# Attention scores from rounded and rest parts in two fp32r products, and six modulation blocks moved to the second layer's attention

## The chip, the cores and the metric

The kernel runs on one core of a Trainium2 chip. The metric is the device time of one execution in microseconds. Before the change it is 2171.98 us, the median of three runs (2163.36, 2171.98 and 2172.99).

## The reference, cut to what matters

Two layers of a hybrid block work on 256 latent tokens and 256 context tokens of width 1024. Each layer computes a modulation vector from a condition, mixes tokens with an attention of eight heads of 64 and a gated delta recurrence of four heads of 128, and ends in a feed-forward part: dense in the first layer, a mixture of eight experts in the second. Everything is fp32.

```python
m_l = (jax.nn.silu(c) @ w_mod[l] + b_mod[l])[:, None, :]      # 6 x 1024 per layer, from 1024 x 6144 weights
m_c = (jax.nn.silu(c_ctx) @ w_mod[l] + b_mod[l])[None, None, :]
sh1, sc1, g1, sh2, sc2, g2 = jnp.split(m_l, 6, axis=-1)
...
s_loc = einsum(q_blk, k_blk) * scale + bias                   # a latent query sees 256 latent keys with a bias
s_ctx = einsum(q_blk, kc) * scale                             # and 256 context keys
p = softmax(concatenate([s_loc, s_ctx], -1))
...
s = einsum('bqhd,bkhd->bhqk', q, k) * (q.shape[-1] ** -0.5)   # context queries: 256 context keys, first layer only
```

The six parts of the modulation are used at different places: the first two ahead of the mixer, `g1` at its end, `sh2` and `sc2` behind it, and `g2` at the end of the feed-forward part. Of the second layer, blocks 0 to 5 of 512 columns hold the first three parts and blocks 6 to 11 the last three.

## The kernel before, in words

Activations are held transposed, with a feature on each partition, as two fp32r tiles for the rounded part and the rest. Weights come in loads of 1 MB through SP's DMA queue into one of three buffers (`raw`), are split by ScalarE (rounding, L90) and VectorE or GpSimd (rest, L91) into fp32r pairs (`ws`, two buffers), and are multiplied in three fp32r products (`mm3`): high times low, high times high, low times high.

A mixer does this work. The projections of the recurrence (`heads`) and of the attention (`fill_pair` for q and k, `fill_tok` for v and z) go through PSUM tiles of tag "acc" (two buffers). The recurrence needs a triangular inverse: `triangles`, a `substitution` of 31 steps on VectorE and GpSimd, `doubling` with small products, and then the steps `recur` and `delta_out`, which load kx, vt, qT and IN from DRAM through SP. `attention` runs per head and per tile of 128 queries: the score product (`sps`, tag "acc"), the bias and scale, maximum and exponential on VectorE and ScalarE, four transposes (`ptp`, tag "tp", two buffers), a copy to SBUF (`pt`), and the product with v (`aop`, tag "m" with one buffer in the second layer, "tp" in the first). The first layer has eight heads times four query tiles, two with 512 keys and two with 256; the second layer has eight heads times two tiles with 512 keys.

A modulation block (`mod_block`) loads two pieces of 1 MB without splitting them, multiplies them in 16 recorded fp32 products into a PSUM tile of tag "m", copies that on ScalarE (`mev`), transposes it in four products (`mt`, the same tag) and reduces it on VectorE. Four blocks run at the very beginning. The other 20 stand in `mod_queue`, and `mod_next` takes the next one, or nothing once the queue is empty. It is called for each of six pairs of the recurrence's projections in the first layer, for each of the 16 steps of the first layer's attention, and at several places of the dense part.

The order of the work is made in three stages. `drive` steps the recurrence and the doubling in turns, and after each turn takes a number of units from one generator, `stream`, that holds the projections, the attention (one unit per head and pair of query tiles) and z; what is left over is taken after them. The emitted order gives each instruction a priority. The framework then simulates a timeline with its own costs and gives each engine a fixed order from it: the first in priority of those that are ready. Buffers are given out by that simulation too. On the chip each engine, and SP's queue, goes strictly through its list.

SBUF tiles of 512 fp32 elements come from one pool (`big`, 48 buffers of 2 KB a partition, L175). The MoE's fifteen load buffers lie partly on the addresses of this pool and of those behind it; a load into one of them waits until what lay there has been read.

Lines that the steps below touch: `mod_queue` and the pool (L173 to L175), `fill_pair` (L404 to L413), the score product (L859), `aop` (L876), the call behind each head (L883 to L885), and the calls in the dense part (L1110, L1135, L1140).

Of the kernel before, what the change touches and what calls it, by code (L numbers as in the profile page):

```python
# [9 lines left out]
F32 = mybir.dt.float32  # L10
F32R = mybir.dt.float32r
I32 = mybir.dt.int32
AF = mybir.ActivationFunctionType
ALU = mybir.AluOpType
# [4 lines left out]
P = 128  # L19
# [35 lines left out]
class Kern:  # L55
# [78 lines left out]
    def run(self):  # L134
        nc, tc, I = self.nc, self.tc, self.I
        with ExitStack() as top:
            self.const = c = self.pool(top, "const")
            self.dram = top.enter_context(tc.tile_pool(name="scr", bufs=1, space=DRAM))
            self.cst = c.tile([P, 5, P], F32, name="cst")
            self.st = self.pool(top, "st", bufs=4)  # L140
            self.raw = self.pool(top, "raw", bufs=3)
            self.wsp = self.pool(top, "wsp", bufs=2)
            self.ps = self.pool(top, "ps", bufs=2, space=PSUM)
            pre = top.enter_context(ExitStack())
            early = self.pool(pre, "early")
            cT = early.tile([P, KD, 32], F32, name="cT")
            nc.vector.memset(cT, 0.0)
            craw = early.tile([P, KD, 2], F32, name="craw")
            nc.scalar.dma_start(craw, I["c"])
            nc.scalar.dma_start(self.cst, I["cst"])  # L150
            self.ident = self.cst[:, 0]
            self.tri = (self.cst[:, 1], self.cst[:, 2])
            self.stri = (self.cst[:, 3], self.cst[:, 4])
            nc.scalar.activation(cT[:, :, 0:2], craw, AF.Silu)
            self.cT = cT
            self.bm = early.tile([P, 2, 48], F32, name="bm")
            nc.scalar.dma_start(self.bm, I["b_mod"])
            self.rope = early.tile([P, 2, 2, 128], F32, name="rope")
            self.lnT = c.tile([P, 4, 2, KD], F32, name="lnT")
            nc.scalar.dma_start(self.lnT, I["lnT"])  # L160
            self.mods = [c.tile([P, 48, 2], F32, name=f"mod{l}") for l in range(2)]
            self.mhalf = c.tile([P, 16], F32, name="mhalf")
            nc.vector.memset(self.mhalf, -0.5)
            one = c.tile([P, 1], F32, name="one")
            nc.vector.memset(one, 1.0)
            self.ones = one.broadcast_to([P, P])
            self.pads = [early.tile([P, 2, 260], F32, name=f"pad{i}") for i in range(2)]
            for t in self.pads:
                nc.vector.memset(t[:, :, 0:2], 0.0)
                nc.vector.memset(t[:, :, 258:260], 0.0)  # L170
            self.x1_d = self.dram.tile([4, P, D], F32, name="x1d")
            self.x2_d = self.dram.tile([4, P, D], F32, name="x2d")
            self.mod_queue = [(0, n) for n in range(4, 12)] + [(1, n) for n in range(12)]  # L173
            with pre:
                self.pb = self.pool(pre, "big", bufs=48)  # L175
                self.pt = self.pool(pre, "tr", bufs=7)
                self.pc = self.pool(pre, "ch", bufs=4)
                self.pd = self.pool(pre, "db", bufs=6)
                self.pa = self.pool(pre, "at", bufs=2)
                self.pr = self.pool(pre, "ro", bufs=2)  # L180
                X = self.xtiles()
                xt = [[self.big(name="xt") for _ in range(2)] for i in range(4)]
                nc.gpsimd.dma_start(self.rope, I["rope"])
                steps = [self.xpose_mod(*self.mod_cols(0, 0, w), w, xt[2 * w : 2 * w + 2], X) for w in range(2)]

                for hf in range(2):
                    for n in (hf, 2 + hf):
                        self.mod_block(0, n)
                    for j in ((0, 1), ())[hf]:
                        for i in range(4):  # L190
                            nc.sync.dma_start(xt[i][j], I["xtok"][i][:, 512 * j : 512 * j + 512])
                        if j == 0:
                            self.first = list(self.wsplit(self.load(I["w_in"][0, 2]), eng=[nc.gpsimd] * 2))
                    for _ in range(4):
                        for t in steps:
                            next(t)
                X2, tail = self.mixer(0, X, None)
                X, tail = self.ffn(X2, tail)
                x1, ab = self.mixer(1, X, tail, top)
            self.moe(x1, ab)  # L200
# [78 lines left out]
    def mixer(self, l, X, tail, keep=None):  # L279
# [4 lines left out]
        with ExitStack() as mx:  # L284
# [117 lines left out]
            ftag, lo = ["g"], [None, None]  # L402

            def fill_pair(pair):  # L404
                to, w = (qa, NT * P) if pair < 8 else (ka, 512)
                r = self.load(I["w_in"][l, pair])
                t2 = self.big((P, 2, 256), name="qk") if w == 256 else None
                for j, hl in enumerate(self.wsplit(r, eng=lo)):
                    acc = wblock(hl, 0, w, ftag[0])
                    t = self.big((P, w), name="qk") if t2 is None else t2[:, j]  # L410
                    nc.scalar.copy(t, acc[:, 0:w])
                    to[2 * (pair % 2) + j] = t
                    yield  # L413

            def fill_tok(which, ch, nt):
# [430 lines left out]
    def attention(self, l, heads, tl, qaT, kaT, VA, na):  # L846
        nc = self.nc
        for h in heads:
            hp = slice(64 * (h % 2), 64 * (h % 2) + 64)
            hs = slice(64 * h, 64 * h + 64)  # L850
            if tl[0] == 0:
                bias = self.inp([P, 2, 256], "bias")
                nc.sync.dma_start(bias, self.I["rpb"][l, h])
            for i in tl:
                c0 = 0 if i < 2 else 256
                w = 512 - c0
                nk = w // P
                sp = self.pst("acc", name="sps")[:, 0:w]
                self.mm(sp, qaT[h // 2][hp, i * P : (i + 1) * P], kaT[h // 2][hp, c0:512], start=True, stop=True)  # L859
                st = self.st.tile([P, 4], F32, name="st", tag="st")  # L860
                pr = self.s2([P, 512], name="pr")
                if i < 2:
                    nc.vector.scalar_tensor_tensor(pr[:, 0:256], sp[:, 0:256], 0.125, bias[:, i], ALU.mult, ALU.add)
                    nc.scalar.activation(pr[:, 256:512], sp[:, 256:512], AF.Copy, scale=0.125)
                    nc.vector.tensor_reduce(st[:, 0:1], pr, AX.X, ALU.max, negate=True)
                    nc.scalar.activation(pr, pr, AF.Exp, bias=st[:, 0:1], accum_out=st[:, 1:2])
                else:
                    nc.vector.tensor_reduce(st[:, 0:1], sp, AX.X, ALU.max)
                    nc.vector.tensor_scalar(st[:, 2:3], st[:, 0:1], -0.125, None, ALU.mult)
                    nc.scalar.activation(pr[:, 0:w], sp, AF.Exp, scale=0.125, bias=st[:, 2:3], accum_out=st[:, 1:2])  # L870
                tp = self.pst("tp", (P, 4, P), name="ptp")
                for j in range(nk):
                    nc.tensor.transpose(tp[:, j], pr[:, j * P : (j + 1) * P], self.ident)
                pt = self.pa.tile([P, 4, P], F32, name="pt", tag="a")
                nc.any.tensor_copy(pt[:, 0:nk], tp[:, 0:nk])
                op = self.pst("m" if l else "tp", (P, 64), name="aop")  # L876
                vs = slice(64 * (h % 4), 64 * (h % 4) + 64)
                for j in range(nk):
                    kt = 4 - nk + j
                    self.mm(op, pt[:, j], VA[kt // 2][:, kt % 2, vs], start=j == 0, stop=j == nk - 1)  # L880
                nc.vector.reciprocal(st[:, 3:4], st[:, 1:2])
                nc.vector.tensor_scalar(na[i][:, hs], op, st[:, 3:4], None, ALU.mult)
            if l == 0:  # L883

                self.mod_next()  # L885
            yield

# [184 lines left out]
    def ffn(self, X, tail):  # L1072

        nc, I = self.nc, self.I
        m = self.mods[0]
        for half in range(2):
            H = []
            for f in range(11):
# [28 lines left out]
                nc.scalar.activation(sg, accs[0], AF.Silu)  # L1107
                nc.vector.tensor_tensor(sg, sg, accs[1], ALU.mult)
                self.split(H[f][0], H[f][1], sg)
                if f % 2:  # L1110
                    self.mod_next()
            if half == 0:
                xs = self.rows(self.x1_d, range(4))
                gr = [self.row(0, 40, w, lambda hf: self.big(name="gr")) for w in range(2)]
# [2 lines left out]
            for w in (None,) if half == 0 else (1, 0):  # L1117
# [4 lines left out]
                for hf in range(2):  # L1122
                    tags = (("acc", "acc", "tp", "tp"), ("g", "g", "g", "tp"))[hf] if w is None else ("acc", "g")[hf : hf + 1] * 2
                    acc = [self.pst(t, name="dacc") for t in tags]
                    for sl in range(3):
                        wd = 2048 if sl < 2 else 1536
                        r = self.load(I["w_dn"][half, hf, :, 2048 * sl : 2048 * sl + wd])
                        for j, (wh, wl) in enumerate(self.wsplit(r, wd)):
                            for q in range(min(2, wd // 512 - 2 * j)):
                                k = 4 * sl + 2 * j + q  # L1130
                                s = slice(512 * q, 512 * q + 512)
                                for a, i in zip(acc, tl):
                                    h = [t[:, i * P : (i + 1) * P] for t in H[k]]
                                    self.mm3(a, *h, wh[:, s], wl[:, s], k == 0, k == 10)
                        if sl:  # L1135
                            self.mod_next()
                    for n, (a, i) in enumerate(zip(acc, tl)):
                        self.residual(xs[i][hf], a, gr[i // 2][hf], 1.0 if half else ALPHA, st[n][:, hf] if half else None)
                if w == 1:
                    self.mod_next(12)  # L1140
                    run(steps)
        return X2, steps

# [730 lines left out]
```

## Time and profile before

| | |
|---|---|
| median of three runs | 2171.98 us |
| profiled execution | 2169.23 us, of which the span of the trace is 2167.4 us |
| TensorE matmul / weight load busy | 2009.4 us (93%) / 1382.7 us (64%) |
| VectorE / ScalarE / GpSimd busy | 1174.2 (54%) / 833.3 (38%) / 245.9 us (11%) |
| mean granted TensorE clock | 0.954 of full speed |
| DMA | 539.94 MB, mean 249 GB/s |

The span falls into these parts: the first layer's projections and inverse to about 240 us, its attention with the recurrence to 426, its output and the dense part to about 900, the second layer's mixer to about 1216, and the mixture of experts to the end. Matmuls are pipelined, so a busy time of TensorE is the union of records that each contain some latency. A granted clock of 1.00 is 2.4 GHz throughout a stretch, 0.50 would be 1.2 GHz throughout it.

### The profile page before, as it was taken

The numbers are of one execution on the slowest core, as the hardware profiler recorded it, in microseconds if no ns is written. First come the engines' busy times: TensorE is split into PE (matmuls) and PEld (weight loads), VectorE is DVE, ScalarE is ACT, GpSimd is POOL, SyncE is SP. The second block draws the span as 40 slices with busy tenths as digits, with TensorE's granted clock in tenths as the row PEclk, the third lists the DMA queues.
The fourth block names the chain that finished last, engine by engine and source line by source line (L and its number), as shares of the span: only waits on it lengthen the run. The fifth ranks groups of instructions, "written<-read, shape, count | busy, mean of one in ns | idle before, by whom it ended". The sixth has DMA issues, their size and how long they took to land. (4 is left out here: it accounts for less than half of the span.)

```text
span 2167.4 us, 29352 instructions
## 1 busy us (share of the span) xinstructions
PE 2009.4 (93%) x11334; PEld 1382.7 (64%) x11334; DVE 1174.2 (54%) x1980; ACT 833.3 (38%) x1312; POOL 245.9 (11%) x276
## 2 busy tenths in 40 slices
PE   7989999998999999898899889999999999998996
PEld 3678766777888887677768663555544445554553
DVE  3777455676324337867765671544344444455565
ACT  2454333443322234454344450433233434435451
POOL 1422200114000000536311000000000000000000
PEclk9999999898999999998789999999999999999998
DMA  8355387453323225334323689999999989989884
GB/s 325 129 192 159 134 308 289 151 203 102 135 93 109 97 91 185 109 111 129 111 76 117 270 349 405 426 427 426 427 374 405 412 325 427 367 317 425 328 333 167
DMA packets 121029, 539.94 MB, mean 249 GB/s; under 512 B 28560, under 2 KB 40912, under 8 KB 62512
## 3 DMA queue, kind: packets, MB, share of 16 engines
q1 hardware_dynamic: 118704, 532.35, 63.9%
q0 software_dynamic: 1600, 5.20, 0.7%
q8 instruction: 91, 1.49, 0.3%
q14 instruction: 58, 0.48, 0.1%
q10 hardware_dynamic: 576, 0.42, 0.1%
HBM read 520.10 MB, written 17.83 MB: 248 GB/s over the span
## 5 line engine op out<-in xcount | busy, mean ns | idle before, releaser
L91 DVE TENSOR_TENSOR ws<-raw,ws 128x1024 fp32r<-128x1024 f32 (+1 forms) x384 | 461.5, 1224 | 261.9 <-ACT ws L90 260.7
L90 ACT CAST ws<-raw 128x1024 fp32r<-128x1024 f32 (+1 forms) x404 | 412.8, 1043 | 338.9 <-PE ga L75 102.2
L75 PE MATMUL ga<-ws,xe 128*128 128x512 f32 x1008 | 261.8, 416 | 32.4 <-DVE ws L91 32.4
L75 PE MATMUL ga<-raw,xr 128*32 128x512 f32 (+1 forms) x1568 | 261.2, 601 | 0.7 <-ACT xr L1371 0.7
L75 PEld LDWEIGHTS ga<-ws,xe 128*128 128x128 f32 x1008 | 195.6, 198 | 100.0 <-DVE ws L91 40.0
L75 PE MATMUL facc<-xh,ws 128*128 128x512 f32 (+1 forms) x736 | 224.0, 386 | 1.9 <-DVE ws L91 1.8
L75 PE MATMUL acc<-xh,ws 128*128 128x512 f32 (+1 forms) x672 | 202.8, 385 | 8.0 <-DVE ws L91 5.4
L75 PEld LDWEIGHTS facc<-xh,ws 128*128 128x128 f32 x736 | 139.6, 193 | 28.9 <-DVE ws L91 2.6
L75 PEld LDWEIGHTS ga<-raw,xr 128*32 128x32 f32 (+1 forms) x1568 | 69.7, 121 | 138.0 <-issue 129.8
L75 PEld LDWEIGHTS acc<-xh,ws 128*128 128x128 f32 x672 | 129.5, 205 | 34.2 <-DVE ws L91 6.1
L75 PE MATMUL facc<-xl,ws 128*128 128x512 f32 (+1 forms) x368 | 143.0, 389 | 2.0 <-ACT ws L90 1.5
L75 PE MATMUL acc<-xl,ws 128*128 128x512 f32 (+1 forms) x336 | 131.5, 391 | 10.4 <-ACT va L435 5.9
L75 PE MATMUL dacc<-ws,Hh 128*128 128x512 f32 x352 | 109.3, 392 | 2.8 <-DVE ws L91 2.8
L75 PE MATMUL y<-ws,hh 128*128 128x512 f32 x336 | 107.5, 401 | 0.0
L1574 POOL TENSOR_TENSOR mv<-mv,mhalf 128x1 f32<-128x1 f32 x2 | 2.0, 993 | 891.0 <-DVE mv L1573 889.2
L75 PE MATMUL yf<-raw,hr 128*32 128x512 f32 (+1 forms) x560 | 93.5, 616 | 2.5 <-ACT hr L1754 2.5
L75 PEld LDWEIGHTS acc<-xl,ws 128*128 128x128 f32 x336 | 69.0, 205 | 26.9 <-ACT va L435 6.3
L75 PE MATMUL acc<-ws,xh 128*128 128x256 f32 x448 | 83.2, 286 | 0.0
L91 DVE TENSOR_TENSOR hl<-tp,hh 128x512 fp32r<-128x512 f32 x21 | 14.5, 692 | 125.5 <-ACT hh L90 125.4
L75 PEld LDWEIGHTS facc<-xl,ws 128*128 128x128 f32 x368 | 71.3, 194 | 16.4 <-ACT ws L90 2.1
L75 PEld LDWEIGHTS dacc<-ws,Hh 128*128 128x128 f32 x352 | 65.1, 188 | 17.6 <-DVE ws L91 4.2
L75 PEld LDWEIGHTS y<-ws,hh 128*128 128x128 f32 x336 | 62.9, 190 | 21.0 <-DVE ws L91 4.1
(372 smaller groups left out, 3005.6 us busy)
## 6 DMA issues: line engine op xcount, KB each, us to landing
raw<-in_m_gu_dram SPq DMA_DIRECT2D x224, 1024.0 KB, 12.3
raw<-in_m_dn_dram SPq DMA_DIRECT2D x112, 1024.0 KB, 13.4
raw<-in_w_mod_dram SPq DMA_DIRECT2D x44, 1024.0 KB, 4.9
raw<-in_w_in_dram SPq DMA_DIRECT2D x28, 1024.0 KB, 5.1
raw<-in_w_gu_dram SPq DMA_DIRECT2D x22, 1024.0 KB, 4.8
raw<-in_w_out_dram SPq DMA_DIRECT2D x12, 1024.0 KB, 4.8
raw<-in_w_dn_dram SPq DMA_DIRECT2D x12, 1024.0 KB, 4.9
raw<-in_w_dn_dram SPq DMA_DIRECT2D x6, 768.0 KB, 4.3
```

The source lines that it names most:

```text
L75: self.next(self.nc.tensor.matmul(*a, **k))
L90: eng.tensor_copy(hi, src) if both else self.nc.scalar.copy(hi, src)
L91: (eng or self.nc.vector).tensor_tensor(lo, src, hi.bitcast(F32), ALU.subtract)
L1574: nc.gpsimd.tensor_tensor(mv[:, 1:2], mv[:, 1:2], self.mhalf[:, 0:1], ALU.pow)
```

## The change

The score of one head becomes two fp32r products that accumulate into the same PSUM tile. For a k tile (two heads, 64 features each, on the two halves of the partitions) `fill_pair` now makes two tiles, one for each head: the rounded part of the head on its own half, the rest on the other half. For a q tile it makes three: for each head the rounded part on both halves, and a third with the rests of both heads on their own halves. The first product contracts over 128 partitions (rounded q times rounded k, and rounded q times the rest of k), the second over 64 (the rest of q times rounded k). The product of the two rests is left out. The copies are ScalarE's, the subtractions VectorE's.

The `big` pool gets 57 buffers instead of 48. The tile `aop` takes tag "tp" in both layers. The modulation queue is drawn on differently: the first layer's attention takes a block behind a head only while more than six are left, and behind each odd head only while more than twelve are left; the second layer's attention takes one behind each head. The calls in the dense part are gone.

```diff
-                self.pb = self.pool(pre, "big", bufs=48)
+                self.pb = self.pool(pre, "big", bufs=57)
...
             def fill_pair(pair):
-                to, w = (qa, NT * P) if pair < 8 else (ka, 512)
+                q = pair < 8
+                to, w = (qa, NT * P) if q else (ka, 512)
                 r = self.load(I["w_in"][l, pair])
-                t2 = self.big((P, 2, 256), name="qk") if w == 256 else None
+                halves = (slice(0, 64), slice(64, 128))
+                small = w == 256
+                both = [self.big((P, 2, 256), F32R, name="qk") for _ in range(3)] if small else None
                 for j, hl in enumerate(self.wsplit(r, eng=lo)):
                     acc = wblock(hl, 0, w, ftag[0])
-                    t = self.big((P, w), name="qk") if t2 is None else t2[:, j]
-                    nc.scalar.copy(t, acc[:, 0:w])
-                    to[2 * (pair % 2) + j] = t
+                    n = 3 if q else 2
+                    ts = [both[m][:, j] if small else self.big((P, w), F32R, name="qk") for m in range(n)]
+                    for m in range(2):
+                        mine, other = halves[m], halves[1 - m]
+                        t, a = ts[m], acc[mine, 0:w]
+                        nc.scalar.copy(t[mine], a)
+                        if q:
+                            nc.scalar.copy(t[other], a)
+                        rest = ts[2][mine] if q else t[other]
+                        nc.vector.tensor_tensor(rest, a, t[mine].bitcast(F32), ALU.subtract)
+                    to[2 * (pair % 2) + j] = ts
                     yield
...
-                self.mm(sp, qaT[h // 2][hp, i * P : (i + 1) * P], kaT[h // 2][hp, c0:512], start=True, stop=True)
+                q, k, tok = qaT[h // 2], kaT[h // 2][h % 2], slice(i * P, (i + 1) * P)
+                self.mm(sp, q[h % 2][:, tok], k[:, c0:512], start=True, stop=False)
+                self.mm(sp, q[2][hp, tok], k[hp, c0:512], start=False, stop=True)
...
-                op = self.pst("m" if l else "tp", (P, 64), name="aop")
+                op = self.pst("tp", (P, 64), name="aop")
...
-            if l == 0:
+            if l == 1 or len(self.mod_queue) > 6 and (h % 2 == 0 or len(self.mod_queue) > 12):
                 self.mod_next()
...
-                if f % 2:
-                    self.mod_next()
...
-                        if sl:
-                            self.mod_next()
...
-                    self.mod_next(12)
                     run(steps)
```

## Rows read from the trace of the kernel before

**Rows 1.** Busy us: PE, PEld, DVE, ACT, POOL; granted clock, DMA share, GB/s.
```profile
268.00:414.00 146.00, 146.00 (x1230) 97.97 (x1229) 81.73 (x245) 57.23 (x149) 9.24 (x13) 1.00 0.76 278
414.00:426.00 12.00, 9.41 (x49) 7.85 (x47) 5.69 (x16) 3.81 (x9) 1.64 (x1) 0.63 0.01 1
...
1000.00:1040.00 40.00, 34.36 (x243) 32.62 (x241) 37.08 (x71) 14.48 (x24) 28.07 (x43) 0.90 0.43 133
1040.00:1072.00 32.00, 25.88 (x230) 23.32 (x230) 23.17 (x52) 14.57 (x39) 10.23 (x10) 0.69 0.41 123
1072.00:1120.00 48.00, 43.71 (x322) 32.50 (x322) 25.61 (x67) 18.59 (x46) 5.28 (x8) 0.74 0.28 88
1120.00:1143.00 23.00, 23.00 (x213) 17.98 (x213) 18.25 (x49) 11.52 (x29) 2.40 (x4) 1.00 0.05 13
...
1220.00:1240.00 20.00, 15.48 (x95) 12.76 (x94) 13.05 (x45) 10.46 (x18) 2.53 (x7) 0.83 0.99 410
1240.00:1260.00 20.00, 13.43 (x51) 10.50 (x50) 15.39 (x28) 9.28 (x10) 0.54 (x1) 0.83 0.58 220
```

**Rows 2.** Timeline of TensorE, first layer's attention: start us, duration us.
```profile
363.67 0.60 PE L227 MATMUL mt<-cst,mev 128*128 128x128 f32 x4
364.11 1.28 PE L75 MATMUL sp<-vn,kx 128*128 128x128 f32 x10
...
366.54 1.92 PE L75 MATMUL mps<-raw,cT 128*32 128x512 f32 x16
368.40 1.13 PE L75 MATMUL sps<-qk 64*128 64x256 f32 x4
369.45 0.56 PE L75 MATMUL qt<-YT,NP 64*64 64x64 f32 x6
...
375.49 1.98 PE L75 MATMUL sps<-qk 64*128 64x512 f32 x4
377.40 0.71 PE L75 MATMUL op<-vn,IN 128*128 128x128 f32 x4
```

**Rows 3.** Timeline of TensorE: fp32r products, dense layer and z.
```profile
523.25 0.39 PE L75 MATMUL facc<-xl,ws 128*128 128x512 f32 x1
...
523.93 0.39 PE L75 MATMUL facc<-xl,ws 128*128 128x512 f32 x1
...
1144.01 0.40 PE L75 MATMUL acc<-ws,xh 128*128 128x256 f32 x2
...
1144.37 0.40 PE L75 MATMUL acc<-ws,xh 128*128 128x256 f32 x2
```

**Rows 4.** Groups by line and shape, ScalarE then VectorE.
```profile
L411 ACT COPY qk<-acc 128x512 f32<-128x512 f32 x12 | 6.8, 595 | 5.0 <-PE acc L75 4.9
...
L411 ACT COPY qk<-acc 128x256 f32<-128x256 f32 x4 | 1.4, 372 | 8.3 <-PE acc L75 8.3
...
L91 DVE TENSOR_TENSOR hl<-tp,hh 128x512 fp32r<-128x512 f32 x21 | 14.5, 692 | 125.5 <-ACT hh L90 125.4
...
L91 DVE TENSOR_TENSOR xe<-gp,xe 128x256 fp32r<-128x256 f32 x12 | 4.8, 420 | 4.2 <-ACT xe L90 4.2
```

**Rows 5.** Timeline of TensorE, tail of the first layer's attention.
```profile
420.08 1.97 PE L75 MATMUL aop<-va,pt 128*128 128x64 f32 x8 [0.73 <-ACT pt L875]
```

**Rows 6.** Timeline of SP's DMA issues, both layers.
```profile
329.74 30.66 SPq L98 DMA_DIRECT2D raw<-in_w_mod_dram  x8
...
1043.13 0.34 SPq L98 DMA_DIRECT2D raw<-in_w_in_dram  x1
1046.67 0.35 SPq L98 DMA_DIRECT2D raw<-in_w_out_dram  x1
...
1081.55 12.54 SPq L318 DMA_DIRECT2D qd<-cv  x2
...
1094.70 0.40 SPq L736 DMA_DIRECT2D kx<-kd  x1
```

**Rows 7.** Timeline of SP's DMA issues, start of the MoE's loads.
```profile
1166.57 13.31 SPq L98 DMA_DIRECT2D raw<-in_m_gu_dram  x2
```

## The prediction

> **What bounds the kernel now.** I read four views in this order: the busy table by stretches, then TensorE's timeline in the first layer's attention, then the DMA queue of SP, then the groups of ScalarE and VectorE copies.
>
> The table by stretches [rows 1] shows two very different attentions. In the first layer's (268 to 414 us) TensorE is busy for 146.00 of 146.00 us at a granted clock of 1.00, VectorE for 81.73 and ScalarE for 57.23; DMA is at 0.76. Every one of the 14 modulation blocks that this attention carries, every score and every step of the recurrence goes through that one full queue. After it comes a short tail (414 to 426) with 9.41 of 12 us busy, one head's softmax chain after another. In the second layer's attention (1040 to 1143) TensorE is busy for 25.88 of 32 us, 43.71 of 48 and 23.00 of 23, with the clock at 0.69, 0.74 and 1.00: about 10.4 us idle, and a clock between the two levels, so part of the busy time runs at 1.2 GHz. DMA is at 0.41, 0.28 and 0.05 there. Just before (1000 to 1040) VectorE is the full engine, 37.08 of 40 us: the triangular substitution.
>
> So the change takes work from a stretch that has no hole and puts some of it into one that has holes. I therefore count removed TensorE time in layer 0 nearly in full, and added or removed TensorE time in layer 1 at about half.
>
> **The scores.** Two fp32 products of 512 columns (four records) hold the queue from 375.49 to 377.40, 0.955 us each; two of 256 columns from 368.40 to 369.45, 0.525 us each [rows 2]. The new form is two fp32r products. Three fp32r products of 512 columns take 0.68 us (523.25 to 523.93), 0.227 us each; three of 256 columns take 0.36 us (1144.01 to 1144.37), 0.12 us each [rows 3]. A new score is then 0.45 or 0.24 us, plus what a change of operand costs between groups; the old figures contain that and the new don't. With all of it lost the saving would be 0.50 and 0.285 us, with 0.2 us a pair kept 0.40 and 0.185. I take 0.45 and 0.235, the middle. Layer 0 has 16 products of each width (8 heads; two local tiles with 512 keys, two context tiles with 256): 16 x 0.45 + 16 x 0.235 = 11.0 us. Layer 1 has 16 of 512: 7.2 us.
>
> **The moved blocks.** A block's 16 products hold TensorE from 366.54 to 368.40, 1.86 us, and its four transposes from 363.67 to 364.11, 0.44 us [rows 2]: 2.30 us. Reading the conditions: the queue holds 14 blocks when layer 0's attention begins; the new test lets 8 through (heads 0, 1, 2, then every even one), and six go to the first six of layer 1's eight heads. 6 x 2.30 = 13.8 us leave layer 0 and arrive in layer 1, with twelve loads of 1 MB. The calls removed in the dense layer find an empty queue already: 6 blocks go with the projections and 16 calls follow in the attention, for 20 blocks. They cost and save nothing.
>
> Layer 0 in sum: 11.0 + 13.8 = 24.8 us less in a full queue. Its bounds are 24.8 and 0 (0 if the queue is only full because it waits in the right places). I take 22, near the row that says full, and leave 3 us to the softmax and recurrence chains that come out from under it: they are next, and the tail of 12 us stays.
>
> Layer 1: +13.8 if each block lands in a full stretch (1120 to 1143), 0 if in the 10.4 idle us before. Nothing in a block waits for the attention, only for its weights, so the planner can put it into gaps; but it is emitted with heads 0 to 5, some of which lie behind 1120. I take +7. The scores there give 0 to -7.2; I take -3.5 for the same reason.
>
> **The operands q and k.** A k tile costs one more ScalarE copy and two VectorE subtractions: 0.595 + 2 x 0.692 = 1.98 us (the 512-column rows; I use the full-partition durations for the half-partition ones). A q tile in layer 0 costs three more copies and two subtractions, 3.17 us; in layer 1 with 256 columns 3 x 0.372 + 2 x 0.420 = 1.96 us [rows 4]. Four k and four q tiles a layer: 20.6 and 15.8 engine-us. They sit between a projection and the release of its accumulator, of which there are two. A projection of 512 columns takes 24 x 0.227 = 5.4 us, longer than 3.2, so in layer 0 TensorE has the other accumulator to go on with: 0. In layer 1 two of the four q tiles fall into the substitution, where VectorE is full: 2 x 2 x 0.42 = 1.7 us, and a little goes to later waits on the accumulators, whose tag the scores share. I take +2, bounds 0 and 15.8.
>
> **The PSUM tile of the attention's output** moves from the single "m" bank to the two "tp" banks in layer 1, since the blocks need "m". The next head's transposes then wait for the copy of the last. Where nothing else is queued that costs 0.73 us a tile (the wait in the tail of layer 0, [rows 5]); 16 tiles make 11.7 us at most, 0 at least, and not below, since a bank is given up. The stretch 1120 to 1143 has other work throughout: +1.
>
> **The loads.** SP issues in order, and a load stands until one of three weight buffers is free. In layer 0 eight modulation loads held SP for 30.66 us, 3.83 each [rows 6]. Behind such a load in layer 1 stand the q spill, the bias, and kx and vt of the recurrence. At present z's and w_out's loads are taken at 1043.13 and 1046.67, long before use, and SP has already stood once for 12.54 us on the spills of q, after which kx goes out at 1094.70. The twelve loads come ahead of z's in the program, so they take the place of idle prefetch, and at DMA shares of 0.05 to 0.41 the bytes are no matter. I take 0, bounds 0 and what the last rival says.
>
> **Nine more buffers** (48 to 57) nearly match the added tiles, 12 in layer 0 and 8 in layer 1. They free nothing for certain; once q and k are dead the w_out splits may start earlier (up to -4). They also move the addresses that the MoE's load buffers reuse: its second weight load stands inside a 13.31 us issue already at 1166.57 [rows 7]. If the first loads came later, the initial fill would be late by some us, but DMA falls from 0.99 to 0.58 between 1220 and 1260 because all buffers are full [rows 1]: 20 x 0.42, about 8 us of slack. I take 0, bounds -4 and +5.
>
> **Sum:** -22 + 7 - 3.5 + 2 + 1 = -15.5 us. What follows is late by as much as the mixer: the dense layer is TensorE's, the MoE begins when the mixer ends. The sum stands against the profiled execution, 2169.23 us (span 2167.4), which gives 2153.7; that execution is 2.75 us under the median of the three, inside their spread. I predict 2154.
>
> **Rivals.**
> First: a full TensorE row that isn't a full engine. The matmul row counts pipelined products with their latency; weight loads fill only 97.97 of 146 us [rows 1]. If the recurrence sets the pace of that stretch, layer 0 gives perhaps 10 us and layer 1 takes 6.5: 2166. Against it: in layer 0 the same chains run beside twice the attention, and TensorE has no hole. The Trainium skill ("Perfetto Trace Analysis", Identifying the Most-Contended Engine) says just this: judge TensorE by weight-load share, not by matmul busy time. By it the stretch would have a third of headroom, and this rival would be the forecast; the trace agrees that the two rows differ, and can't say which binds.
>
> Second: the moved blocks hold the clock up. At 0.69 over 32 us and 0.74 over 48, some 45 us lie at the lower level, 87% of them busy: 39 us of work that would take 19.5 at the upper one. If the blocks fill the gaps (0 instead of +7) and 8 us come back: -22 - 0.5 - 8, 2139. For it: gaps and lower clock stand together in [rows 1]; against: the gaps there are waits on VectorE, and six blocks are few. The Trainium skill ("TensorE: Matmul & The Clock Gate", What's actually happening) has it that activity releases the throttle; by it this rival would hold.
>
> Third, the slower side: SP's stands hit the recurrence of layer 1. Three of its steps load kx and vt after 1090. If each stands behind three modulation loads at 3.83 us, 34.5 us are added to a chain that has no cover there, the blocks themselves being hidden by that wait: -22 + 34.5 + 2 = +14.5, 2184. It decides from about 20 us of stands on. For it: kx already waits for SP once. Against: the blocks wait for nothing but weights, so buffers come free quickly.
>
> Fourth: the change doesn't spread the blocks. The order is planned on a simulated timeline; the six may be drawn together before the first head or to the end, at full price: -22 + 13.8 - 3.5 + 3 = -8.7, 2160.5.
>
> **How the numbers follow.** Forecast 0.48 (own range 2143 to 2161), first rival 0.19, second 0.14, third 0.13, fourth 0.06. About what a measurement of this kernel can tell from no change is 0.5%, 11 us. Faster by more: the forecast but for its edge (0.45), the second, and edges of the first and fourth (0.04): 0.63. Within: the first and fourth in the main, and edges: 0.25. Slower: the third: 0.12. The range 2135 to 2179 leaves out part of the second and most of the third.
>
> **What would show it.** Right: the first layer's attention ends some 20 us before 414, still with a full TensorE row; score records become fp32r ones of 512 and 256 columns at about 0.23 and 0.12 us; six blocks between 1020 and 1150 of the old count, and the distance from the substitution's end to z's projection up by 3 to 8 us. Wrong: holes on TensorE in the first attention (first rival), a granted clock near 1.00 after 1040 (second), SP stands of over 10 us ahead of kx or vt in layer 1 (third). A changed length of the dense layer or the MoE would mean that I missed a part.

## The result and the profile after

The changed kernel takes 2184.29 us (median of 7 runs, 2179.06 to 2185.52) against 2168.93 us (7 runs, 2163.24 to 2172.99) beside it on the same chips: a ratio of 1.0068, 95% interval 1.0054 to 1.0083. It is slower by 0.7%, and 2154 was predicted. Its profiled execution took 2179.06 us (span 2177.3), the quickest of the seven, so the spans below show 10 us of the 15.

The groups of TensorE by tile give marks that cut the span: the first score, the first product of the first layer's output projection (`wacc<-ws`), the end of the second layer's decays (`dacc<-xh,wbl`) and the last product of its output projection (`wacc<-wo`). Of the changed kernel, with durations min/median/max in ns, then first and last start:
```profile
L75 PE MATMUL sps<-qk x96: 362/492/796, 279.7 to 1148.8; 128*128 128x512 f32 x32, 64*128 64x512 f32 x32, 128*128 128x256 f32 x16, 64*128 64x256 f32 x16
...
L75 PE MATMUL wacc<-ws,m x192: 387/393/499, 423.9 to 482.2; 128*128 128x512 f32 x192
L75 PE MATMUL wacc<-wo,m x96: 387/389/628, 1193.5 to 1220.7; 128*128 128x512 f32 x96
...
L75 PE MATMUL dacc<-xh,wbl x24: 276/282/432, 23.6 to 892.1; 128*16 128x256 f32 x16, 128*16 128x512 f32 x8
```
Five stages follow from them, here for all kernels profiled (us; the experiments' names are explained below):
```
                     to first  first      to 2nd   second  MoE and
                     score     attention  decays   mixer   end
before               267.8     159.3      470.9    316.8   952.6
after                279.7     144.2      468.2    328.6   956.6
e1 scores            280.4     168.6      470.7    321.6   957.3
e2 blocks            270.5     138.2      470.3    321.0   951.1
e3 buffers           267.9     157.1      470.7    311.8   957.8
e4 rows128           280.7     130.4      471.1    323.5   955.5
e5 no rests          268.1     119.8      470.7    315.0   (959.7)
e6 rests GpSimd      289.2     126.6      470.1    317.9   957.2
e7 rests SBUF        282.5     128.9      470.1    318.9   956.7
e8 fp32, k zeros     273.3     131.8      468.6    320.2   959.9
e9 fp32, q zeros     268.2     133.5      470.4    321.1   954.4
e10 q alone          268.0     127.3      469.0    317.9   (1121.7)
e11 k alone          275.8     121.9      470.0    318.0   (958.5)
e12 eight blocks     267.7     134.5      469.9    323.9   954.9
e13 late k, GpSimd   281.0     125.5      470.0    322.3   959.9
e14 late k, VectorE  283.1     127.2      470.2    324.9   959.6
e15 one product      267.9     125.5      470.4    308.5   961.2
```
The first attention is 15.1 us shorter, but it starts 11.9 us later; the second mixer is 11.8 us longer; the MoE grew by 4.0.

Busy time by stretches of the changed kernel, columns as in [rows 1]:
```profile
120.00:140.00 20.00, 16.41 (x85) 11.61 (x84) 18.50 (x51) 14.33 (x36) 0.00 (x0) 0.91 0.73 214
...
160.00:180.00 20.00, 13.79 (x66) 10.10 (x65) 17.71 (x47) 3.25 (x5) 10.95 (x21) 0.74 0.52 179
...
279.70:289.70 10.00, 6.09 (x42) 4.38 (x42) 5.17 (x15) 5.44 (x12) 2.27 (x3) 0.67 0.64 210
289.70:299.70 10.00, 10.00 (x61) 7.40 (x63) 3.57 (x12) 2.40 (x9) 0.00 (x0) 0.50 0.01 2
300.00:412.00 112.00, 112.00 (x958) 82.77 (x951) 75.03 (x211) 47.69 (x126) 7.82 (x11) 1.00 0.59 219
```
From 300 on the attention is as full as in [rows 1]. Larger are the holes ahead of it (3.6 and 6.2 us in the first two rows; the kernel before has 0.2 and 2.8 there), and new is the one at its start: TensorE is idle for 3.9 of 10 us, and for the next 10 us the granted clock is 0.50, which is 1.2 GHz. Up to the first score TensorE is idle for 32.6 us, 7.7 more than before. Another 1.9 of the 11.9 us are 14 products of a block that now stand ahead of the first score (270.75 to 272.60), where they stood behind it.

Who held TensorE, from the waits between 100 and 292 us, then between 940 and 1060 (engine, tile and line, what it waited for: us in total, times, longest):
```profile
PE acc L75 <- DVE qk L424: 2.8, 1, 2.8
PE ptp L889 <- ACT pr L886: 2.8, 1, 2.8
```
```profile
PE acc L75 <- DVE qk L424: 5.7, 1, 5.7
PE ctp L336 <- ACT cv L333: 5.7, 2, 3.7
PE qt L75 <- DVE YT L630: 4.2, 1, 4.2
```
L424 is the subtraction of the rest parts. Its groups, with the two copies L420 and L422, between 100 and 300 us:
```profile
L424 DVE TENSOR_TENSOR qk<-acc,qk 64x512 fp32r<-64x512 f32 x16 | 11.0, 688 | 2.7 <-ACT qk L422 2.3
...
L420 ACT CAST qk<-acc 64x512 fp32r<-64x512 f32 x16 | 9.3, 580 | 15.5 <-PE acc L75 13.9 <-DVE qk L424 1.3
...
L422 ACT CAST qk<-acc 64x512 fp32r<-64x512 f32 x8 | 4.6, 580 | 0.1
```
And VectorE's timeline shows where the last of k's subtractions stand, between steps of the triangular substitution (L608, L609) and other casts:
```profile
144.87 0.19 DVE L608 TENSOR_TENSOR tm<-UX 128x31 f32<-128x31 f32 x1 [2.78 <-ACT UX L521]
...
146.28 0.68 DVE L424 TENSOR_TENSOR qk<-acc,qk 64x512 fp32r<-64x512 f32 x1
147.00 0.42 DVE L609 TENSOR_TENSOR UX<-UX,tm 128x87 f32<-128x87 f32 x1
...
147.79 1.21 DVE L91 TENSOR_TENSOR ws<-raw,ws 128x1024 fp32r<-128x1024 f32 x1
...
150.24 0.69 DVE L424 TENSOR_TENSOR qk<-acc,qk 64x512 fp32r<-64x512 f32 x1
```

The longest wait in the hole at the attention's start, 2.8 us, is for `pr`, the exponential of the first head (L886). ScalarE's timeline has the copies of the last q tile, and an instruction that loads a table, ahead of it:
```profile
283.05 0.58 ACT L420 CAST qk<-acc 64x512 fp32r<-64x512 f32 x1
283.64 0.58 ACT L422 CAST qk<-acc 64x512 fp32r<-64x512 f32 x1
284.25 1.28 ACT L886 ACT_TABLE_LOAD   x1
285.54 0.47 ACT L886 ACTIVATE pr<-sps,st 128x256 f32<-128x256 f32 x1
```

The score itself, against [rows 2]: TensorE's timeline and that of its weight loads around one score of 512 columns:
```profile
382.17 0.90 PE L75 MATMUL sps<-qk 128*128 128x512 f32 x2
383.01 0.49 PE L75 MATMUL sp<-vn,kx 128*128 128x128 f32 x2
```
```profile
382.15 0.19 PEld L75 LDWEIGHTS sps<-qk 128*128 128x128 f32 x1
382.58 0.18 PEld L75 LDWEIGHTS sps<-qk 64*128 64x128 f32 x1 [0.25 <-issue]
383.00 0.30 PEld L75 LDWEIGHTS sp<-vn,kx 128*128 128x128 f32 x2 [0.24 <-issue]
```
The two products hold the queue for 0.84 us, not 0.45. The load of the second starts 0.41 us after the first product, not beside it, and the next load over 128 rows waits in the same way. Three products of one kind in [rows 3] took 0.227 us each.

### The profile page after: what moved, and what is told of

It is laid out like the page before. It is cut to its first block, busy times and chain, and to the rows that moved or that the text cites. A ratio compares the mean times of both kernels' runs of the same rounds, so it can differ in the third digit from the quotient of the medians.

```text
span 2177.3 us, 29402 instructions
## 1 busy us (share of the span) xinstructions
PE 2000.4 (92%) x11334; PEld 1377.1 (63%) x11334; DVE 1192.6 (55%) x2011; ACT 848.0 (39%) x1345; POOL 246.7 (11%) x276
```

## The experiments

Each is timed in five rounds beside the kernel before. The theory I began with: operands and scores cost, blocks pay. The rivals: stands of SP, the buffers, the planner's other order. From e4 on, every form with two products a score has e4's edit too.

**e1: operands and scores without the moved blocks** (57 buffers, `fill_pair` and the score products as changed; conditions, removed calls and the bank of `aop` as before).

> The kernel before with the new operands and scores and 57 buffers; the modulation blocks stay where they were. My theory after the result: the copies and subtractions of q and k hold the two projection accumulators and delay the first layer's scores by about 12 us, cost some 6 more in the second layer, and the scores themselves give nothing back (0.84 us a pair against 0.955 for 512 columns, 0.62 against 0.525 for 256): 2182 to 2192 us, first layer's first score near 280, its attention as long as before (159 us). Rival: the moved blocks and their loads cost the time in the second layer, and the scores gain what was predicted: 2155 to 2165.

2201.04 us, ratio 1.012 (1.0095 to 1.0144). That is above even the expected range. The rival falls: without any moved block the time is worse still. The attention did not stay at 159 but grew to 168.6, with the hole at its start and half the clock behind it:
```profile
280.40:290.40 10.00, 6.05 (x45) 4.32 (x42) 5.17 (x15) 5.45 (x12) 2.28 (x3) 0.68 0.73 234
290.40:300.40 10.00, 10.00 (x61) 7.47 (x64) 3.57 (x12) 2.48 (x9) 0.00 (x0) 0.50 0.01 2
```

**e2: the moved blocks alone** (the conditions, the removed calls and the bank of `aop` as changed; all else as before).

> The kernel before with only the moved blocks (and the attention's output in the two tp banks in the second layer). My theory: the first layer's attention gets 14 us shorter, the second layer's mixer 7 to 12 longer, nothing else moves: 2162 to 2168 us. Rival (stands of SP on weight loads reach the second layer's recurrence): second mixer 20 us and more longer, 2175 to 2190.

2152.69 us, ratio 0.9903 (0.9879 to 0.9928): below the expected range, and faster than both kernels with all parts of the arithmetic kept. The first attention is 21.1 us shorter, which is more than the 13.8 that six blocks were priced at, and the second mixer 4.2 us longer. Summed from each product's start to the next one's, the products and transposes of the blocks hold TensorE in the first attention for 15.6 us less (36.9 before, 21.3 here). The rest fits the clock of the tail (last column but two), which is 0.63 in [rows 1] and 1.00 here:
```profile
394.50:408.70 14.20, 13.20 (x117) 12.46 (x115) 11.75 (x24) 4.49 (x11) 4.55 (x3) 1.00 0.01 1
```
Stretches of its second attention (columns as in [rows 1]):
```profile
1040.00:1060.00 20.00, 19.19 (x208) 16.04 (x206) 14.22 (x38) 6.85 (x21) 3.43 (x7) 0.83 0.25 85
1060.00:1105.00 45.00, 41.32 (x320) 26.07 (x319) 22.77 (x66) 17.51 (x41) 3.00 (x4) 0.85 0.61 228
```
The blocks fill gaps, and the granted clock is 0.83 and 0.85 where [rows 1] has 0.69 and 0.74. That the blocks raise it isn't shown, though: over the whole second mixer the clock is higher than before by as much in e3 (below), which moves no block. The rows are of before, e2 and e3:
```profile
898.00:1214.80 316.80, 281.54 (x1897) 236.96 (x1895) 219.39 (x467) 140.37 (x279) 100.92 (x106) 0.88 0.36 117
```
```profile
879.00:1200.00 321.00, 290.07 (x2017) 233.30 (x2015) 221.20 (x483) 141.96 (x284) 99.71 (x106) 0.91 0.44 154
```
```profile
895.70:1207.50 311.80, 276.90 (x1897) 233.13 (x1895) 220.88 (x467) 139.93 (x279) 98.83 (x106) 0.91 0.35 113
```
No long stand of SP shows in the length of this mixer.

**e3: 57 buffers alone** (`bufs=48` to `bufs=57`).

> The kernel before with 57 instead of 48 buffers and nothing else. My theory: the MoE's first weight loads find their addresses free later, and its own length grows by 4 us as in the changed kernel: 2172 to 2175, mixers unchanged. Rival: the MoE's 4 us come from the mixer's later end alone: 2167 to 2170.

2169.27 us, ratio 0.9993 (0.9979 to 1.0007): no change. In its profile the MoE is 5.2 us longer and the second mixer 5.0 shorter. So the buffers are not to blame for the total; whether the 4 us of the changed kernel's MoE are theirs or chance is not settled, since MoE lengths from 951 to 961 occur among kernels that did not touch it. The 5.0 us of the second mixer also say how far a single execution can be trusted there.

**e4: the second product over 128 rows.**
```diff
-                self.mm(sp, q[2][hp, tok], k[hp, c0:512], start=False, stop=True)
+                self.mm(sp, q[2][:, tok], k[:, c0:512], start=False, stop=True)
```


> The changed kernel with the second product of a score over all 128 rows instead of 64 (it then adds the neighbour head's rest part, which is not wanted). Theory: a weight load is not hidden where the number of active rows changes, which costs about 0.2 us at each of two changes: a score pair of 512 columns falls from 0.84 to 0.45 to 0.6 us, the first layer's attention from 144 to 136 to 139 us, total 2174 to 2179. Rival: the load is exposed for another reason (fp32 neighbours, waits), and the pair stays at 0.84, total 2182 to 2186.

2162.80 us, ratio 0.995 (0.9929 to 0.9972), 21.5 us under the changed kernel, and well under the expected range, for one edited line that makes the product read more. TensorE's products stand in the same order in both traces, so the planner's order is no rival here. Its timeline:
```profile
381.37 0.72 PE L75 MATMUL sps<-qk 128*128 128x512 f32 x2
381.93 0.55 PE L75 MATMUL aop<-va,pt 128*128 128x64 f32 x4
```
A pair falls from 0.84 to between 0.54 and 0.67 us, and the attention from 144.2 to 130.4. Summed from start to start, all scores of the first attention hold TensorE for 25.3 us before, 24.6 after, 15.4 here. So 9.2 of the 13.8 us are the scores'. The rest fits the clock: the hole at the start is here too, but the 10 us behind it have a granted clock of 0.97 (second row), where the changed kernel has 0.50.
```profile
280.70:290.70 10.00, 5.87 (x50) 5.16 (x48) 5.52 (x17) 5.99 (x12) 2.28 (x3) 0.69 0.70 235
290.70:300.70 10.00, 10.00 (x117) 7.91 (x117) 5.75 (x22) 4.57 (x16) 0.00 (x0) 0.97 0.39 139
```
(What the added rows contribute is a product of two rest parts, as small as the one that the change itself leaves out.)

**e5: without the operands' work.**
```diff
-                    (copies and subtractions of the two halves)
+                    t = both[0][:, j] if small else self.big((P, w), F32R, name="qk")
+                    nc.scalar.copy(t, acc[:, 0:w])
+                    ts = [t] * n
```


> Both score products over 128 rows, but q and k evacuated as in the kernel before, by one whole copy a tile (rounded; the rest parts are left out, so the scores are of lower precision), 48 buffers. My theory: what is left of the operands' cost goes: the first layer's first score falls from 280.7 back to 268 to 271 us, the second layer's mixer gets 3 to 5 us shorter, the MoE's length goes back by 3 to 4: 2140 to 2147 us. Rival (the late first score comes from the planner's other order, not from the copies): first score stays at 278 to 281, 2156 to 2163.

2127.21 us, ratio 0.9799 (0.9783 to 0.9815). Scores mix two heads here, which lets the MoE choose other experts; this run, e10 and e11 are read only up to the second mixer's end (brackets in the table).
```profile
L75 PE MATMUL sps<-qk x96: 278/396/796, 268.1 to 1097.1; 128*128 128x512 f32 x64, 128*128 128x256 f32 x32
...
L75 PE MATMUL wacc<-ws,m x192: 387/391/504, 387.9 to 446.7; 128*128 128x512 f32 x192
```
The first score is back at 268.1, the first attention ends 23.2 us earlier than in e4, and the second mixer is 8.5 us shorter. That is what the operands cost. (The nine buffers are gone too, but alone, in e3, they shortened these two stages, by 2.1 and 5.0 us.)

**e6 and e7: the accumulator released by one copy**, the parts made from SBUF, the subtractions on GpSimd (e6) or VectorE (e7).
```diff
+                    raw = self.s2([P, w], name="raw_qk")
+                    nc.scalar.copy(raw, acc[:, 0:w])
-                        t, a = ts[m], acc[mine, 0:w]
+                        t, a = ts[m], raw[mine]
-                        nc.vector.tensor_tensor(rest, a, ...)
+                        nc.gpsimd.tensor_tensor(rest, a, ...)
```


> Both score products over 128 rows with the rest parts kept; one ScalarE copy releases the projection's accumulator, the rounded halves are copied from that copy, and the subtractions run on GpSimd. If VectorE, full in the substitution, is what the subtractions cost: first score at 269 to 274 us, total 2145 to 2154. If the copies on ScalarE or the later operands are the cost: first score stays near 280, total 2158 to 2166.

> As the kernel before it in this list, with the subtractions on VectorE, from the SBUF copy. If the held accumulators are the cost (the step that the prediction put at nothing): first score at 269 to 274 us, total 2145 to 2154. If it is VectorE's time in the substitution: first score near 280, total 2158 to 2168.

2168.62 us (0.9996, 0.9983 to 1.0009) and 2159.48 us (0.9948, 0.9929 to 0.9967), first scores at 289.2 and 282.5. Neither a held accumulator nor VectorE alone explains the late start: released at once, or with GpSimd in VectorE's place, it stays. Neither form relieves ScalarE, which makes one copy a tile more here.

**e10 and e11: only q, or only k, in parts**; the other is evacuated by one whole copy.

> Both products over 128 rows; q is split as in the changed kernel, k is evacuated by one whole rounded copy (its rest parts are left out, and the neighbour head's rows enter the scores). If the k tiles' copies and subtractions in the substitution are what delays the first layer: first score at 268 to 273 us, total 2136 to 2146. If the q tiles' are: first score at 278 to 281, total 2152 to 2160.

> The other half: k is split as in the changed kernel, q is evacuated by one whole rounded copy (its rest parts are left out, and the neighbour head's rows enter the scores). If the k tiles are the cost: first score at 276 to 281 us, total 2147 to 2158; if the q tiles are: first score at 268 to 272, total 2132 to 2142.

2294.99 and 2149.82 us, which say little (e10's MoE alone takes 1121.7 us). The marks do say something:
```profile
L75 PE MATMUL sps<-qk x96: 278/397/792, 268.0 to 1112.2; 128*128 128x512 f32 x64, 128*128 128x256 f32 x32
```
```profile
L75 PE MATMUL sps<-qk x96: 278/393/792, 275.8 to 1115.7; 128*128 128x512 f32 x64, 128*128 128x256 f32 x32
```
With q alone in parts (first row) the start is on time and the attention 7.5 us longer than in e5; with k alone (second row) the start is 7.7 late and the attention 2.1 longer. To the attention's end that is 7.4 and 9.8 us, together less than the 23.2 of both at once. Of the two it is the form with q in parts that has the hole at the attention's start; the first 10 us of the attention in e10, then in e11:
```profile
268.00:278.00 10.00, 6.74 (x54) 6.34 (x53) 5.93 (x17) 5.92 (x13) 2.28 (x3) 0.71 0.64 210
```
```profile
275.80:285.80 10.00, 10.00 (x104) 6.54 (x104) 7.48 (x26) 5.98 (x16) 2.91 (x3) 1.00 0.78 288
```

**e13 and e14: k split after the substitution**, from a whole fp32 copy, rest parts on GpSimd (e13) or VectorE (e14).
```diff
+            def split_k():
+                for n in range(4):
+                    raw, ts = ka[n], [self.big((P, 512), F32R, name="qk") for _ in range(2)]
...
-                    yield from zipped(heads(0), vas)
+                    yield from zipped(heads(0), [one(ks), one(ks), vas[0], one(ks), one(ks), vas[1]])
```


> Both products over 128 rows, all parts kept; a k tile leaves its accumulator by one whole fp32 copy as in the kernel before and is split only after the substitution, with the heads that follow (rounded halves by ScalarE, rest parts by GpSimd, from SBUF). If the place of k's splitting, in the queue of the substitution, is what delays the first layer: first score at 268 to 273 us, first layer's end 10 to 13 us earlier than with k split at once (411), total 2146 to 2154. If it is the amount of work wherever it stands: first score at 276 to 282, total 2158 to 2166.

> The same with k's rest parts by VectorE, which is busy for about 11 of 20 us there. If the place is the cost, the engine doesn't matter: within 4 us of the GpSimd form, 2146 to 2156. If VectorE's time is what counts: 2156 to 2166, first score at 274 to 282.

2156.71 (0.995, 0.9934 to 0.9967) and 2169.56 us (1.0008, 0.9997 to 1.0019); first scores at 281.0 and 283.1, the attention's end at 406.5 and 410.3 against 411.1. My theory that the place in the substitution is the cost falls: the same work costs nearly as much behind it. Of the two engines GpSimd was the better one by 13 us in time.

**e8 and e9: the moved blocks with fp32 scores over 128 rows**, by zeros in the other head's half of the k tiles (e8, 52 buffers) or of the q tiles (e9, 48).
```diff
+                            nc.gpsimd.memset(t[m][other], 0.0)
+                            nc.scalar.copy(t[m][mine], acc[mine, 0:w])
-                self.mm(sp, qaT[h // 2][hp, ...], kaT[h // 2][hp, c0:512], start=True, stop=True)
+                self.mm(sp, qaT[h // 2][h % 2][:, ...], kaT[h // 2][:, c0:512], start=True, stop=True)
```


> The moved blocks alone, with fp32 scores whose k tiles carry zeros in the other head's 64 rows, so that a score runs over 128 rows like its neighbours. If a change of the number of rows exposes a weight load in fp32 too: a score of 512 columns falls from 1.00 to about 0.88 us, of 256 from 0.58 to 0.46, the first attention from 138 to 134 us, total 2146 to 2150, less the added copies (up to 4). If only fp32r products pay for it: 1.00 and 0.58 stay, total 2153 to 2158.

> The moved blocks with fp32 scores over 128 rows, the zeros now in the q tiles (the k tiles, which are evacuated during the substitution, keep one whole copy) and 48 buffers. If the changed row count is what an fp32 score pays for too: first score at 268 to 272 us, first attention 131 to 133 us, total 2144 to 2149. If the copies of q eat it: 2150 to 2156.

2156.29 (0.9941, 0.9924 to 0.9958) and 2151.89 us (0.992, 0.9904 to 0.9935): no better than e2, though their first attentions are 6.4 and 4.7 us shorter. All scores there hold TensorE for 22.9 and 23.4 us against 26.1 in e2, so an fp32 score gains less from equal rows than a pair of fp32r products does (9.2 us).

**e12: eight blocks to the second layer** (`> 6` to `> 8`).

> The moved blocks alone, fp32 scores as before, but eight blocks go to the second layer, one with each of its eight heads. In the run with six, a block taken out gave 3.5 us in the first attention and cost 0.7 us in the second layer. If that goes on: 5 to 6 us less than with six, 2146 to 2149 us. If the second layer's gaps are filled by six: the last two cost 2 to 4 us each there, 2152 to 2156.

2158.64 us (0.9954, 0.9936 to 0.9972). The first layer gains another 6.5 us to its end, the second mixer loses 2.9, and the time is no better than with six.

**e15: one product a score.** As e9, with fp32r tiles: q and k rounded once.

> The moved blocks with a single fp32r product a score over 128 rows (zeros in the q tiles), q and k rounded once and no rest parts (left out). What the scores could give at most: a pair of about 0.32 us for 512 columns, first attention 112 to 118 us, first score at 268 to 271, first layer's end at 381 to 388 us. If the products are not what the attention pays for, the attention stays at 128 to 133 us.

2133.32 us, ratio 0.9831 (0.9814 to 0.9848), the fastest of the forms that keep the heads apart, at the lower precision. My bound for its attention failed: 125.5 us, where 112 to 118 was expected and e5 has 119.8 with two products. Its scores hold TensorE for 9.7 us against 14.7 in e5, and none of that came back. What sets the length here is open; TensorE is busy for 109.63 of the first 110.10 us.

## Why the prediction was wrong

The profiles before, e2, e5, e4 and after form a chain in which each step is one part of the change (the nine buffers go with the operands). To the end of the first attention, and in the second mixer (us; each a difference of single executions, and e3's 5.0 us in the second mixer warn that no single step of that column is shown by itself):
```
                              first layer          second mixer
                          predicted  measured   predicted  measured
blocks and aop's bank       -13.8     -18.4       +8         +4.2
scores as priced            -11.0     -20.8       -3.5       -6.0
operands q and k              0       +23.2       +2         +8.5
second product on 64 rows     -       +12.8       -          +5.1
sum                         -22 *      -3.2       +6.5      +11.8
```
(* 24.8, of which 22 was taken.)

**The step that failed is the operands':** "so in layer 0 TensorE has the other accumulator to go on with: 0". The amount was right: 20.6 engine-us foretold; 11.0 of VectorE and 13.9 of ScalarE are there, in place of the 4.8 of eight plain copies at the 595 ns of [rows 4]. The cover was not. I compared one tile's 3.2 us with one projection's 5.4, as if the two engines stood ready. In the trace the copy and the subtraction of a half each queue behind substitution steps and weight casts, the projections come later, the softmax of the first head waits with nothing beside it, and the clock falls to 1.2 GHz in the hole. e5 and e4 price it at 23 us, more than the engine time itself. Which queue carries most of it stays open: a released accumulator (e7), GpSimd (e6) and a later place (e13, e14) each left the first score at 281 us or later, and none of these forms relieved ScalarE.

**The second failure is in the scores' price.** I wrote that the new figure lacks "what a change of operand costs between groups" and spoke of 0.2 us a pair; the sum took less, for 0.40 and 0.185 leave only 0.1 us of a score's saving to it (0.2 would give 0.305 and 0.085), and the middle that I took 0.05. It is 0.4: with 64 rows in one product and 128 in its neighbours neither load is hidden, and e4 shows it by changing the rows alone. The 12.8 us of that row aren't all the scores', as e4 says: between 4 and 5 fit the lower clock behind the hole. With equal rows the term was right: 25.3 us of scores before, 14.7 in e5, 10.6 less where 11.0 was predicted. That e5's first attention is shorter than e2's by 18.4 us, 7 more than its scores account for, lies in part in what the old scores cost their neighbours: four transposes ahead of a 64-row score hold the queue for 0.53 us in e2, and ahead of a 128-row score for 0.36 in e5 (first and second pair of rows). My prices left that out; the remainder is open.
```profile
329.40 0.60 PE L873 MATMUL ptp<-cst,pr 128*128 128x128 f32 x4
329.93 0.70 PE L75 MATMUL sps<-qk 64*128 64x256 f32 x2
```
```profile
327.93 0.61 PE L883 MATMUL ptp<-cst,pr 128*128 128x128 f32 x4
328.29 0.49 PE L75 MATMUL sps<-qk 128*128 128x256 f32 x2
```

The blocks' term was right in sign and too cautious on both sides: more gain in the first layer, less cost in the second. The first rival (TensorE not really full) falls for the blocks: the 15.6 us that left the queue in e2 came back in time. In e15, where 5 us less of scores gave nothing, it stays open. The second (clock) isn't shown: the second mixer's clock is higher in e2, but as high in e3 without a moved block, and the mixer is 4.2 us longer where I had 8; the 8 us that the rival expected back are not there. The third foretold the right time, 2184, by luck and for a wrong reason: e2 has all the twelve loads and its second mixer is only 4.2 us longer. The fourth did not happen: the six blocks of the changed kernel's second attention begin at 1067, 1087, 1104, 1114, 1124 and 1133 us.

## What to carry to other kernels

Price an operand's preparation by what its engines are doing at that moment and by the chain copy, subtract, release, not by its share of an engine; then look at what TensorE has left to do when it comes late. Before a product is split in two, compare the rows of its stationary tile with those of its neighbours: in e4 64 more harmless rows cost nothing, and the change of rows did. When a change has several parts, time each alone: here the blocks gained 1.0% and the operands and scores lost 1.2%.

## What was new of the hardware

A weight load takes 0.18 us for 64 rows and 0.19 for 128. The Trainium skill ("TensorE: Matmul & The Clock Gate", LDWEIGHTS) says that the number of rows doesn't matter to a load, and the trace agrees. Yet a 512-column fp32r product took 0.41 to 0.43 us where the number of rows changed, 0.32 as the first of a pair in e4, and 0.227 in a row of its own kind.

What exposes the load is the change, not the 64 rows. Between 300 and 412 us of the changed kernel the 16 loads for a score's second product start 0.43 us (median) after the 512-column product over 128 rows that precedes them, and not beside it. Loads over 64 rows behind products over 64 rows start 0.003 us (median of 42) after them, as in this group of TensorE and its loads:
```profile
383.43 0.68 PE L75 MATMUL qt<-YT,NP 64*64 64x64 f32 x8
```
```profile
383.42 0.54 PEld L75 LDWEIGHTS qt<-YT,NP 64*64 64x64 f32 x8
```
The same page of the Trainium skill (The mechanism) says that loads overlap running products only where the row groups differ, though it also lets a load into the background weight buffer be pulled ahead. With the first the trace does not agree: here loads over the same rows run beside the products, and a load over another number of rows waits.

Half the partitions take as long to copy or subtract as all of them: 580 ns on ScalarE and 688 on VectorE for 64 x 512, against 595 and 692 for 128 x 512 in [rows 4].

Four idle microseconds at the start of the attention were followed by 10 us at a granted clock of 0.50, in e1 and in the changed kernel alike; in e4, with a hole as long, the following 10 us had 0.97. Why is open.
